# The expert layer of a decoder block: 64 of 256 tokens through fetched expert rows on VectorE, 64 in a stationary block of high and low parts, 128 as before

## The chip, the cores and the metric

One core of a Trainium2 chip runs the whole kernel in one launch. The metric is the device time of that launch in microseconds. The kernel before takes 2736.85 us (median of 3 runs, 2736.78 to 2737.09). The engines are TensorE (PE in the profile, its weight loads PEld), VectorE (DVE), ScalarE (ACT), GpSimd (POOL) and SyncE (SP), which issues most transfers.

## The reference

A decoder block for 256 tokens of width 2048 in float32: a retention branch and a dilated attention, merged by gates; a cross-attention to 256 memory tokens; and an expert layer of 16384 experts, of which each token takes 16 for each of 8 heads. The change is in the last one:

```
def peer_ffn(h, w_q, subkeys, u_tab, v_tab):
    qh = (ht @ w_q).reshape(t, PEER_HEADS, 2, PEER_QUERY_DIM // 2)
    sc = jnp.einsum('thpd,hpnd->thpn', qh, subkeys)
    v_top, i_top = lax.top_k(sc, PEER_TOPK)
    combo = (v_top[:, :, 0, :, None] + v_top[:, :, 1, None, :]).reshape(...)
    c_val, c_idx = lax.top_k(combo, PEER_TOPK)
    ...
    e_idx = i1 * PEER_N_KEYS + i2
    gates = jax.nn.softmax(c_val, axis=-1)
    ...
        u = u_tab[i_]
        a = jax.nn.gelu(jnp.einsum('td,tkd->tk', x_, u), approximate=False)
        return jnp.einsum('tk,tkd->td', a * g_, v_tab[i_])
```

So each token needs 128 rows of `u_tab` and 128 of `v_tab`, each of 2048 numbers (8 KB). Each table has 134 MB.

## The kernel before, in words

All weights are streamed once from HBM in 464 pieces of 1 MB (128 partitions x 4 k-slices x 512 columns). `ahead` (L960) brings each piece in: SyncE loads it into one of 3 raw buffers, ScalarE rounds it to a high part (`hi`, L967), VectorE subtracts that to get the low part (`lo`, L968, the "split"). The left operand, the activations transposed, is kept in high and low parts too. For each k-slice and each block of 128 tokens `mm3` (L201 to L204) adds three products: high by high, high by low, low by high. So a piece is 4 x 2 x 3 = 24 matmuls. The split runs two pieces ahead of TensorE (`SPLIT_AHEAD`).

The order of everything beside the pieces is written by generators. After each piece `tick` (L120) gives each active generator a credit; a generator runs until its yields have used it up. The credit is `TICK` = 4.0 after each piece, and `FINE` = 1.5 twice a piece while the routing runs (`fine`).

The expert layer does not fetch rows. It computes all 16384 experts densely for all 256 tokens. In 128 pieces of `u` (32 chunks of 512 experts) it multiplies the normalized tokens by the table; `evac_u` (L768) applies the Gelu on ScalarE and GpSimd's queue stores the chunk's activations to HBM. Meanwhile VectorE routes: `route_top` and `route_pairs` select the experts and `gate_matrix` (L737) makes, from one-hot rows (L749, L751) and small matmuls (L758), a matrix G of 256 tokens x 16384 gates, mostly zeros, in HBM. `weigh` (L780) reads G and the activations back chunk by chunk, multiplies them on VectorE (L802) and transposes the product with `to_T`; `v_group` (L805) multiplies that by 128 pieces of `v` and adds the sums to the residual rows `x_rows` (L827). The first 80 pieces are of `u` (`RUN_AHEAD` = 20 chunks), then 8 of `v` and 8 of `u` in turn, at the end `v` alone.

Buffers of 4 KB per partition are called `unit`; there are 29 of them, taken from whatever was given back.

Of the kernel before, what the change touches and what calls it, by code (L numbers as in the profile page):

```python
# [33 lines left out]
SPLIT_AHEAD = 2  # L34
N_UNITS = 29
TICK = 4.0
FINE = 1.5

# [33 lines left out]
def block_kernel(ctx, tc, a, out):  # L72
# [73 lines left out]
    def piece(ap, fn):  # L146
        prog.append((ap, fn))
# [506 lines left out]

    G_d = [dp.tile([128, N_EXP], F32, name=f"G{tb}") for tb in range(2)]
    g_done = []

    rt = [{}, {}]

    def route_top(n):  # L660

        while sc_rows[n] is None:
            yield
        for tb in range(2):
            if n == 0:
                u = unit([3, 256])
                rt[tb]["v"] = u[:, 0].rearrange("p (n a) -> p n a", a=16)
                rt[tb]["i"] = u[:, 1].bitcast(U32).rearrange("p (n a) -> p n a", a=16)
                rt[tb]["if"] = u[:, 2].rearrange("p (h s a) -> p h s a", h=8, s=2)
            for i in range(4):  # L670
                top16(rt[tb]["v"][:, 4 * n + i], rt[tb]["i"][:, 4 * n + i], sc_rows[n][:, tb, i], work([128]))
                yield 1.57
        sc_rows[n] = 0

# [38 lines left out]

    def route_gates():
        yield
        yield
        for tb in range(2):
            ex = rt[tb]["g"][0]
            nc.scalar.activation(ex, ex, AF.Exp)
        for tb in range(2):  # L720
            ex, sel, _ = rt[tb]["g"]
            su = sp.tile([128, 2, 8], F32, tag="gsum", name="gsum")
            nc.vector.tensor_reduce(su[:, 0], ex, axis=AX.X, op=OP.add)
            nc.vector.reciprocal(su[:, 1], su[:, 0])
            nc.vector.tensor_tensor(sel[:, 2], ex, bc(su[:, 1, :, None], [128, 8, 16]), op=OP.mult)
        yield
        for tb in range(2):
            _, sel, uc = rt[tb]["g"]
            tp = bank("tp", [3, 128])
            for s in range(3):  # L730
                nc.tensor.transpose(tp[:, s], sel[:, s].rearrange("p h k -> p (h k)"), ident)
            tt = uc[:, 3:6]
            nc.scalar.copy(tt, tp)
            rt[tb] = {"T": tt}
        yield

    def gate_matrix():  # L737
# [3 lines left out]
        prev = None  # L741
        for tb, t0 in [(tb, t0) for tb in range(2) for t0 in range(0, 128, 8)] + [(None, None)]:
            cur = None
# [18 lines left out]
            yield 2.6  # L762
        fine[0] = False
        g_done.extend([0, 1])

    ga = {}

    def evac_u(c, acc):  # L768
        g = unit([2, 512])
        for tb in range(2):  # L770
            nc.scalar.activation(g[:, tb], acc[tb], AF.Gelu, scale=sm["rstd2"][:, tb:tb + 1])  # L771
        d = dp.tile([128, 2, 512], F32, name=f"act{c}")
        nc.gpsimd.dma_start(d, g)  # L773
        ga[c] = d

    A_T = {}
    v_at = [0]
    y_rows = {}

    def weigh():  # L780

        while len(g_done) < 2:
            yield
        w = {}

        def load(c):
            w[c] = unit([2, 512]), unit([2, 512])
            for tb in range(2):
                nc.sync.dma_start(w[c][0][:, tb], G_d[tb][:, c * 512:c * 512 + 512])
            nc.sync.dma_start(w[c][1], ga.pop(c))  # L790

        yield
        yield
        load(0)
        for c in range(N_CH):
            while (c + 1 < N_CH and c + 1 not in ga) or c > 2 * v_at[0] + 3:
                yield
            if c + 1 < N_CH:
                load(c + 1)
            yield  # L800
            m, g = w.pop(c)
            nc.vector.tensor_mul(g, g, m)  # L802
            yield from to_T(g, A_T, c)

    def v_group(gi):  # L805
        accs = {}
        for n in range(4):
            for c2 in range(2):
                def fn(hi, lo, n=n, c2=c2):
                    c = 2 * gi + c2  # L810
                    v_at[0] = gi
                    wait(lambda: c in A_T)
                    if c2 == 0:
                        accs[n] = [bank("acc", [512]) for _ in range(2)]
                    th, tl = A_T[c]
                    for k in range(4):
                        for tb in range(2):
                            s = slice(tb * 128, tb * 128 + 128)
                            mm3(accs[n][tb], th[:, k, s], tl[:, k, s], hi[:, k], lo[:, k],
                                c2 == 0 and k == 0, c2 == 1 and k == 3)  # L820
                    if n == 3:
                        del A_T[c]
                    if c2 == 1:
                        acc = accs.pop(n)
                        r = x_rows[n]
                        for tb in range(2):
                            nc.vector.tensor_add(r[:, tb], r[:, tb], acc[tb])  # L827
# [92 lines left out]
    def route():  # L920
        for n in range(4):
            yield from route_top(n)
        for tb in range(2):
            yield from route_pairs(tb)
        yield from route_gates()
        yield from gate_matrix()
    call(lambda: add(route()))
    call(lambda: add(weigh()))
    chunks(a["w_pq"], hf_T, KQ, late, evac_rows_T(pq_T, "rstd2"))

    def u_chunk(c):
        chunks(a["u"][c * KQ:c * KQ + KQ], hf_T, KQ, straight(0, 1), lambda _, acc: evac_u(c, acc))

# [125 lines left out]
def _layout(inputs):  # L1059
# [33 lines left out]
```

## Time and profile before

| | |
|---|---|
| median of 3 runs | 2736.85 us |
| the profiled execution: its time, and its span | 2736.54 us, 2734.7 us |
| TensorE busy | 2715.8 us (99%) |
| VectorE busy | 1691.2 us (62%) |
| ScalarE busy | 1160.0 us (42%) |
| GpSimd busy | 116.4 us (4%) |
| granted clock of TensorE, mean | 0.999 |
| bytes moved, mean rate | 580 MB, 212 GB/s |

The expert layer's pieces run from about 1245 us to the end. Three views are used below. The page groups instructions by line: busy time, mean duration, and the idle time of the engine before them with what ended it. The windows give busy time of every engine in a stretch, the share of time that the 16 transfer engines were busy, and GB/s. The timeline shows single instructions; two neighbouring ones of an engine overlap by a little, so what an instruction costs a full engine is the distance of two starts.

### The profile page before, as it was taken

The page shows a single profiled execution, that of the slowest core. Times are in us where ns is not written, and L with a number is a line of the kernel's source. Part 1 is how long each engine was busy: PE and PEld are TensorE (multiplying, and loading weights), DVE is VectorE, ACT ScalarE, POOL GpSimd, SP SyncE. Part 2 cuts the span into 40 slices and gives each one's busy share as a digit, 9 for nine tenths or more (in the row PEclk, how much of TensorE's full clock was granted, in tenths as well). Part 3 has the DMA queues.
Part 4 walks back from the last instruction along what each step waited for, and adds up shares of the span by engine and source line. Part 5 has one row for each costly group of instructions (what it writes and reads, how often), then busy time and mean ns, then how long its engine had stood idle before and what let it go on. Part 6 is the DMA issues. An engine that isn't in the chain of part 4 may idle for free.

```text
span 2734.7 us, 31099 instructions
## 1 busy us (share of the span) xinstructions
PE 2715.8 (99%) x12642; PEld 2266.7 (83%) x12642; DVE 1691.2 (62%) x2115; ACT 1160.0 (42%) x1047; POOL 116.4 (4%) x125
## 2 busy tenths in 40 slices
PE   9999999999999999999999999999999999999998
PEld 7888888888888888888888888888888888888886
DVE  7566447886554444569998885445555455666664
ACT  6444334443464443444445444333344334333333
POOL 1211110002000000000000000000000000000001
PEclk9999999999999999999999999999999999999999
DMA  8554554567575444545667777565666566666663
GB/s 294 193 178 170 187 190 177 193 240 255 187 264 189 171 156 156 183 171 198 218 216 238 241 242 281 211 224 214 223 232 239 206 224 231 248 218 248 233 229 123
DMA packets 127951, 580.48 MB, mean 212 GB/s; under 512 B 11200, under 2 KB 43968, under 8 KB 68928
## 3 DMA queue, kind: packets, MB, share of 16 engines
q1 hardware_dynamic: 118096, 543.23, 56.1%
q0 software_dynamic: 9712, 35.26, 3.4%
q8 instruction: 99, 1.62, 0.2%
q14 instruction: 44, 0.36, 0.0%
HBM read 538.61 MB, written 39.85 MB: 212 GB/s over the span
## 4 chain that ended last, share of the span: by engine, by line
PE 98%; POOL 1%; DVE 1%; issue 0%; DMA 0%; POOLq 0%; SPq 0%; ACT 0%; DVEq 0%
PE acc L202 30%; PE acc L204 30%; PE acc L203 30%; PE tp L185 2%; PE sm L758 2%; POOL unit L332 1%; PE sm L584 1%; PE sm L615 1%; PE sm L456 0%; PE sm L478 0%; DVE work L326 0%; PE sm L640 0%; DVE work L330 0%; DMA raw<-in_w_in_dram 0%; PE tp L472 0%
## 5 line engine op out<-in xcount | busy, mean ns | idle before, releaser
L968 DVE TENSOR_TENSOR lo<-raw,hi 128x2048 fp32r<-128x2048 f32 (+1 forms) x464 | 1060.1, 2286 | 822.7 <-ACT hi L967 819.0
L202 PE MATMUL acc<-hi,unit 128*128 128x512 f32 x3712 | 1458.4, 393 | 6.3 <-ACT hi L987 6.3
L204 PE MATMUL acc<-hi,unit 128*128 128x512 f32 x3712 | 1445.9, 390 | 0.0
L203 PE MATMUL acc<-lo,unit 128*128 128x512 f32 x3712 | 1445.5, 389 | 0.0
L967 ACT CAST hi<-raw 128x2048 fp32r<-128x2048 f32 (+1 forms) x464 | 881.8, 1902 | 885.6 <-PE acc L204 767.9
L202 PEld LDWEIGHTS acc<-hi,unit 128*128 128x128 f32 x3712 | 697.5, 188 | 146.6 <-ACT hi L987 6.3
L204 PEld LDWEIGHTS acc<-hi,unit 128*128 128x128 f32 x3712 | 697.0, 188 | 145.7
L203 PEld LDWEIGHTS acc<-lo,unit 128*128 128x128 f32 x3712 | 697.6, 188 | 141.7 <-DVE lo L988 0.9
L827 DVE TENSOR_TENSOR unit<-unit,acc 128x512 f32<-128x512 f32 x128 | 87.5, 687 | 28.2 <-PE acc L204 27.7
L190 ACT CAST unit<-tp 128x512 fp32r<-128x512 f32 x76 | 40.9, 590 | 142.7 <-PE tp L185 142.7
L191 DVE TENSOR_TENSOR unit<-tp,unit 128x512 fp32r<-128x512 f32 x76 | 48.9, 685 | 75.3 <-ACT unit L190 75.3
L749 DVE TENSOR_SCALAR unit<-iota,unit 128x128 f32<-128x128 f32 x256 | 88.4, 345 | 0.0
L771 ACT ACTIVATE unit<-acc,rstd 128x512 f32<-128x512 f32 x64 | 43.8, 690 | 81.6 <-PE acc L204 81.6
L185 PE MATMUL tp<-ident,unit 128*128 128x128 f32 x544 | 71.8, 273 | 1.4 <-POOL unit L332 1.4
L751 DVE TENSOR_SCALAR unit<-iota,unit 128x128 f32<-128x128 f32 x256 | 73.0, 285 | 0.0
L185 PEld LDWEIGHTS tp<-ident,unit 128*128 128x128 f32 x544 | 63.1, 140 | 11.5 <-POOL unit L332 3.5
L759 ACT COPY unit<-sm 128x512 f32<-128x512 f32 x64 | 37.6, 588 | 79.3 <-PE sm L758 67.3
L773 POOL DMA_DIRECT2D act<-unit x32 | 17.1, 535 | 1109.0 <-ACT unit L771 1109.0
L758 PEld LDWEIGHTS sm<-unit 128*128 128x128 f32 x512 | 62.0, 191 | 2.5
L758 PE MATMUL sm<-unit 128*128 128x128 f32 x512 | 62.2, 275 | 0.0
L389 DVE RECIPROCAL unit<-unit 128x256 f32<-128x256 f32 x32 | 56.1, 1754 | 1.1
L188 ACT COPY unit<-tp 128x512 f32<-128x512 f32 x44 | 23.7, 592 | 59.2 <-PE tp L185 59.2
(183 smaller groups left out, 772.4 us busy)
## 6 DMA issues: line engine op xcount, KB each, us to landing
raw<-in_u_dram SPq DMA_DIRECT2D x128, 1024.0 KB, 4.8
raw<-in_v_dram SPq DMA_DIRECT2D x128, 1024.0 KB, 4.8
raw<-in_w_in_dram SPq DMA_DIRECT2D x96, 1024.0 KB, 4.7
raw<-in_w_kv_dram SPq DMA_DIRECT2D x32, 1024.0 KB, 4.7
raw<-in_w_out_dram SPq DMA_DIRECT2D x16, 1024.0 KB, 4.7
raw<-in_w_qm_dram SPq DMA_DIRECT2D x16, 1024.0 KB, 4.8
raw<-in_w_om_dram SPq DMA_DIRECT2D x16, 1024.0 KB, 4.7
raw<-in_w_pq_dram SPq DMA_DIRECT2D x16, 1024.0 KB, 4.8
```

The source lines that it names most:

```text
L185: nc.tensor.transpose(tp[:, k, tb * 128:tb * 128 + 128], rows[:, tb, f:f + 128], ident)
L191: nc.vector.tensor_sub(lo[:, s], tp, hi[:, s])
L202: nc.tensor.matmul(acc, lh, rh, start=start, stop=False)
L203: nc.tensor.matmul(acc, lh, rl, start=False, stop=False)
L204: nc.tensor.matmul(acc, ll, rh, start=False, stop=stop)
L389: nc.vector.reciprocal(rows[:, tb, c], rows[:, tb, c])
L749: nc.vector.tensor_scalar(cur[0][:, i], iota, it[:, 0, t], it[:, 2, t], op0=OP.is_equal, op1=OP.mult)
L751: nc.vector.tensor_scalar(cur[1][:, i], iota, it[:, 1, t], None, op0=OP.is_equal)
L758: nc.tensor.matmul(p[:, i], lh[:, 4 * j + i], rh[:, 4 * j + i], start=True, stop=True)
L827: nc.vector.tensor_add(r[:, tb], r[:, tb], acc[tb])
L967: nc.scalar.copy(hi[:, ks], raw[:, ks])
L968: nc.vector.tensor_sub(lo[:, ks], raw[:, ks], hi[:, ks])
```

## The change

The 256 tokens are no longer treated alike in the expert layer.

- Tokens 0 to 127 are computed densely as before, with three matmuls per k-slice.
- Tokens 128 to 191 are computed densely with high and low parts side by side in one 128-wide stationary block. `side_by_side` copies the low parts of these 64 tokens into the columns of the high parts of tokens 192 to 255. Per k-slice two matmuls (block by high, block by low) give sums whose upper and lower 64 partitions are added in the evacuation, with a ScalarE copy between partition halves and a VectorE addition (L876, L877 of the changed kernel). `evac_u` now stores from ScalarE's queue, in two parts.
- Tokens 192 to 255 (`LANES`) leave the dense computation. `lanes_in` makes their normalized rows, `lanes` does their experts on VectorE. A token takes two partitions, each with 64 of its 128 experts, and a row is handled in two halves of 1024 numbers, so there are 128 steps for `u` and 128 for `v`. A step fetches 128 half rows, one per partition, by an indirect transfer of GpSimd's queue; it is then one VectorE instruction: a TENSOR_TENSOR_REDUCE for the dot product with the token's row, or a SCALAR_TENSOR_TENSOR that adds the weighted row to the sum. Fetches are issued 3 steps ahead (`ROWS_AHEAD`). A step's yield costs 0.8 of a piece's credit (`LANE_STEP`), so 5 steps go with 4 pieces. The sums come into the residual rows in the last but one group of `v_group`.
- Routing is done for tokens 128 to 255 first, so that the row steps can start; `gate_matrix` has 64 + 128 tokens. There is one more unit buffer.

The diff, cut to what is spoken of:

```
-N_UNITS = 29
+N_UNITS = 30
+LANES = slice(64, 128)
+LOW = slice(0, 64)
+LANE_STEP = 0.8
+ROWS_AHEAD = 3
...
-        for tb, t0 in [(tb, t0) for tb in range(2) for t0 in range(0, 128, 8)] + [(None, None)]:
+        for tb, t0 in [(1, t0) for t0 in range(0, 64, 8)] + [(0, t0) for t0 in range(0, 128, 8)] + [(None, None)]:
...
+    def lanes(sel):
...
+        def fetch(i):
+            if i < 256:
+                rows[i] = unit([1024])
+                t = a["u_rows" if i < 128 else "v_rows"]
+                j = i % 128
+                nc.gpsimd.indirect_dma_start(rows[i], None, t, bass.IndirectOffsetOnAxis(
+                    ap=ix[:, j // 2, j % 2:j % 2 + 1], axis=0))
+
+        def turn():
+            return LANE_STEP * (2 * FINE if fine[0] else TICK)
...
+        for i in range(128):
+            r = rows.pop(i)
+            nc.vector.tensor_tensor_reduce(r, r, hn[i % 2].rearrange("p a b -> p (a b)"), 1.0, 0.0, OP.mult, OP.add,
+                                           dots[:, i // 2, i % 2:i % 2 + 1])
+            del r
+            fetch(i + ROWS_AHEAD)
+            yield turn()
...
+        for i in range(128):
+            r = rows.pop(128 + i)
+            y = ys[i % 2].rearrange("p a b -> p (a b)")
+            nc.vector.scalar_tensor_tensor(y, r, coef[:, i // 2:i // 2 + 1], y, op0=OP.mult, op1=OP.add)
+            del r
+            fetch(128 + i + ROWS_AHEAD)
+            yield turn()
...
     def evac_u(c, acc):
-        g = unit([2, 512])
-        for tb in range(2):
-            nc.scalar.activation(g[:, tb], acc[tb], AF.Gelu, scale=sm["rstd2"][:, tb:tb + 1])
-        d = dp.tile([128, 2, 512], F32, name=f"act{c}")
-        nc.gpsimd.dma_start(d, g)
+        g = work([512])
+        nc.scalar.activation(g, acc[0], AF.Gelu, scale=sm["rstd2"][:, 0:1])
+        d = dp.tile([128, 512], F32, name=f"act{c}")
+        nc.scalar.dma_start(d, g)
         ga[c] = d
+        own, other = (LANES, LOW) if c % 2 else (LOW, LANES)
...
+        nc.scalar.copy(w[own], acc[1][other])
+        nc.vector.tensor_add(w[own], w[own], acc[1][own])
+        nc.scalar.activation(b[own], w[own], AF.Gelu, scale=sm["rstdB"][own])
...
+                for k in range(4):
+                    first, last = kq == 0 and k == 0, kq == KQ - 1 and k == 3
+                    mm3(accs[0], th[:, k, 0:128], tl[:, k, 0:128], hi[:, k], lo[:, k], first, last)
+                    nc.tensor.matmul(accs[1], th[:, k, 128:256], hi[:, k], start=first, stop=False)
+                    nc.tensor.matmul(accs[1], th[:, k, 128:256], lo[:, k], start=False, stop=last)
...
     def v_group(gi):
...
                     for k in range(4):
-                        for tb in range(2):
-                            s = slice(tb * 128, tb * 128 + 128)
-                            mm3(accs[n][tb], th[:, k, s], tl[:, k, s], hi[:, k], lo[:, k],
-                                c2 == 0 and k == 0, c2 == 1 and k == 3)
+                        f, e = c2 == 0 and k == 0, c2 == 1 and k == 3
+                        mm3(accs[n][0], ta[:, 0, k], ta[:, 1, k], hi[:, k], lo[:, k], f, e)
+                        nc.tensor.matmul(accs[n][1], tb[:, k], hi[:, k], start=f, stop=False)
+                        nc.tensor.matmul(accs[n][1], tb[:, k], lo[:, k], start=False, stop=e)
...
+    def side_by_side(kq):
+        hi, lo = hf_T[kq]
+        nc.scalar.copy(hi[:, :, 192:256], lo[:, :, 128:192])
```

How the order moves, at three places. First TensorE in a piece of `u` past the 80th: one k-slice before, where acc_14853 is tokens 0 to 127 and acc_14854 tokens 128 to 255 (unit_7702 holds high parts of the activations, unit_7703 low ones):

```order
L202 MATMUL acc_14853<-hi_14879,unit_7702 128x512
L203 MATMUL acc_14853<-lo_14880,unit_7702 128x512
L204 MATMUL acc_14853<-hi_14879,unit_7703 128x512
L202 MATMUL acc_14854<-hi_14879,unit_7702 128x512
L203 MATMUL acc_14854<-lo_14880,unit_7702 128x512
L204 MATMUL acc_14854<-hi_14879,unit_7703 128x512
```

and the same now (acc_11873 and acc_11874; unit_7703 high, unit_7704 low):

```order
L206 MATMUL acc_11873<-hi_11899,unit_7703 128x512
L207 MATMUL acc_11873<-lo_11900,unit_7703 128x512
L208 MATMUL acc_11873<-hi_11899,unit_7704 128x512
L900 MATMUL acc_11874<-hi_11899,unit_7703 128x512
L901 MATMUL acc_11874<-lo_11900,unit_7703 128x512
```

The sixth matmul is gone; the low parts of tokens 128 to 191 stand in the columns of unit_7703.

Second VectorE in the pieces of `u` and `v` after the routing. Before, the splits (`lo`) stand alone but for a few rows at the end of a group, where `v`'s sums are added (L827) and a chunk is weighted (L802):

```order
L968 TENSOR_TENSOR lo_14513<-raw_14424,hi_14512 128x2048
L968 TENSOR_TENSOR lo_14548<-raw_14456,hi_14547 128x2048
L968 TENSOR_TENSOR lo_14585<-raw_14486,hi_14584 128x2048
L827 TENSOR_TENSOR unit_4861<-unit_4861,acc_14553 128x512
L827 TENSOR_TENSOR unit_4861<-unit_4861,acc_14554 128x512
L802 TENSOR_TENSOR unit_14112<-unit_14112,unit_14111 128x1024
```

Now, with unit_13567 and unit_13568 the two sums of the fetched rows, unit_9055 the weights, and the third name a fetched row:

```order
L1145 TENSOR_TENSOR lo_14162<-raw_14073,hi_14161 128x2048
L877 TENSOR_TENSOR work_14192<-work_14192,acc_14076 64x512
L853 SCALAR_TENSOR_TENSOR unit_13568<-unit_14101,unit_9055,unit_13568 128x1024
L1145 TENSOR_TENSOR lo_14200<-raw_14107,hi_14199 128x2048
L853 SCALAR_TENSOR_TENSOR unit_13567<-unit_14130,unit_9055,unit_13567 128x1024
L853 SCALAR_TENSOR_TENSOR unit_13568<-unit_14159,unit_9055,unit_13568 128x1024
L1145 TENSOR_TENSOR lo_14234<-raw_14136,hi_14233 128x2048
```

One row step, and at every fourth piece two, stands between two splits, and L877, for which ScalarE waits in `evac_u`, stands among them.

Third GpSimd's queue in the same stretch. Before it held the activation stores:

```order
L773 DMA act12_11025<-unit_11022 128x1024 [waits DMASW0_49,Activation_49]
L773 DMA act13_11312<-unit_11309 128x1024 [waits DMASW1_49,Activation_49]
L773 DMA act14_11567<-unit_11564 128x1024 [waits DMASW2_49,Activation_49]
L773 DMA act15_11772<-unit_11769 128x1024 [waits DMASW3_49,Activation_49]
L773 DMA act16_11932<-unit_11929 128x1024 [waits DMASW4_49,Activation_49]
```

Now it holds the fetches of rows:

```order
L824 DMA unit_13812<-in_v_rows_dram,unit_9055 128x1024 [waits DMASW2_49,DVE_49]
L824 DMA unit_13815<-in_v_rows_dram,unit_9055 128x1024 [waits DMASW3_49,DVE_49]
L824 DMA unit_13847<-in_v_rows_dram,unit_9055 128x1024 [waits DMASW4_49,DVE_49]
L824 DMA unit_13889<-in_v_rows_dram,unit_9055 128x1024 [waits DMASW5_49,DMAHW2_49,PE_49,Activation_49]
L824 DMA unit_13921<-in_v_rows_dram,unit_9055 128x1024 [waits DMASW7_49,DMASW6_49,DVE_49]
```

A fetch waits for the engine that last used its unit buffer, mostly VectorE with an earlier row step, at times TensorE or a store.

More of the change, by code (lines that the diff above doesn't have):

```diff
@@ L231, in chunks @@
             piece(wap[n * nk + kq], make(n, kq, c == 0, c == nk - 1))
+            if after is not None and n == 3:
+                call(lambda kq=kq: after(kq))
     def straight(n0, n1, nk=KQ):
@@ L777, in block_kernel, with u_chunk, make, fn @@
+    A_T, B_T = {}, {}
     v_at = [0]
     y_rows = {}
+    def u_chunk(c):
+        accs = []
+        def make(kq):
+            def fn(hi, lo):
+                wait(lambda: "rstdB" in sm)
+                if kq == 0:
+                    accs.extend(bank("acc", [512]) for _ in range(2))
+                th, tl = hf_T[kq]
+                for k in range(4):
[3 more added lines that the diff above has]
+                    nc.tensor.matmul(accs[1], th[:, k, 128:256], lo[:, k], start=False, stop=last)
+                    if k == 1 and fine[0]:
+                        tick()
+                if kq == KQ - 1:
+                    evac_u(c, accs)
+            return fn
+        for kq in range(KQ):
+            piece(a["u"][c * KQ + kq], make(kq))
@@ new lines, in weigh @@
+            A_T[c] = o
+            if c % 2 == 0:
+                continue
+            t = w.pop("b")
+            nc.vector.tensor_mul(t[:, 1], t[:, 1], t[:, 0])
+            yield
+            tp = bank("tp", [4, 128])
+            for k in range(4):
+                nc.tensor.transpose(tp[:, k], t[:, 1, k * 128:k * 128 + 128], ident)
+            o = unit([2, 4, 128], F32R)
+            both = tp.rearrange("p k (c t) -> p c k t", c=2)
+            for j in range(2):
+                nc.scalar.copy(o[:, j, :, 0:64], both[:, j])
+                nc.vector.tensor_sub(o[:, j, :, 64:128], both[:, j], o[:, j, :, 0:64])
@@ L805, in v_group, with evac @@
+            B_T[c // 2] = o
     def v_group(gi):
         accs = {}
+        last = gi == N_CH // 2 - 1
+        def evac(n, acc):
+            r = x_rows[n]
+            nc.vector.tensor_add(r[:, 0], r[:, 0], acc[0])
+            if not last:
+                nc.vector.tensor_add(r[:, 1], r[:, 1], acc[1])
+                if gi == N_CH // 2 - 2:
+                    w = work([512])
+                    nc.scalar.copy(w[LOW], r[LANES, 1])
+                    nc.vector.tensor_add(r[LOW, 1], r[LOW, 1], w[LOW])
+                    wait(lambda: "ys" in sm)
+                    nc.scalar.copy(r[LANES, 1], sm["ys"][n // 2][LANES, n % 2])
+                return
+            w = work([512])
+            nc.scalar.copy(w[LOW], acc[1][LANES])
+            nc.vector.tensor_add(r[LOW, 1], r[LOW, 1], acc[1][LOW])
+            nc.vector.tensor_add(r[LOW, 1], r[LOW, 1], w[LOW])
+            y_rows[n] = unit([2, 512]) if n < 3 else r
+            for tb in range(2):
+                j = work([512])
+                nc.scalar.activation(j, r[:, tb], AF.Square, accum_out=ssq3[:, tb, n:n + 1])
+                if n < 3:
+                    nc.gpsimd.tensor_mul(y_rows[n][:, tb], r[:, tb], g_fin[n // 2][:, n % 2])
@@ L928, in block_kernel @@
     call(lambda: add(weigh()))
[L929 to L932 removed]
+    call(lambda: add(lanes_in()))
+    def side_by_side(kq):
+        hi, lo = hf_T[kq]
+        nc.scalar.copy(hi[:, :, 192:256], lo[:, :, 128:192])
+    chunks(a["w_pq"], hf_T, KQ, late, evac_rows_T(pq_T, "rstd2"), side_by_side)
     call(lambda: fine.__setitem__(0, True))
```

187 lines of the change are left out of this document (129 added, 58 removed).

## The prediction

> **What bounds the kernel now.** I read the page first, then busy time by stage, then single instructions in the stages that the change touches. The page's first lines and its chain of waits:
>
> ```profile
> span 2734.7 us, 31099 instructions
> PE 2715.8 (99%) x12642; PEld 2266.7 (83%) x12642; DVE 1691.2 (62%) x2115; ACT 1160.0 (42%) x1047; POOL 116.4 (4%) x125
> ...
> PE 98%; POOL 1%; DVE 1%; issue 0%; DMA 0%; POOLq 0%; SPq 0%; ACT 0%; DVEq 0%
> PE acc L202 30%; PE acc L204 30%; PE acc L203 30%; PE tp L185 2%; PE sm L758 2%; POOL unit L332 1%; PE sm L584 1%; PE sm L615 1%; PE sm L456 0%; PE sm L478 0%; DVE work L326 0%; PE sm L640 0%; DVE work L330 0%; DMA raw<-in_w_in_dram 0%; PE tp L472 0%
> ```
>
> TensorE is the chain: it hardly waits for anybody, so the time is the number of matmuls times their spacing. The spacing is not the 0.39 us of a row but the distance of two starts. TensorE in the timeline, two rows that are 24 matmuls (one weight piece) apart:
>
> ```profile
> 1786.03 0.39 PE L202 MATMUL acc<-hi,unit 128*128 128x512 f32 x1
> ...
> 1791.47 0.39 PE L202 MATMUL acc<-hi,unit 128*128 128x512 f32 x1
> ```
>
> 5.44 us for 24, 0.2267 us each. The expert layer has 256 of the 464 pieces. I cut its time where the changed program's order changes character: 65 pieces with routing and gate matrix (stage A, 1245 to 1660 us of before), 160 pieces (stage B, to 2551), the rest (stage C). Busy time by stage:
>
> ```profile
> core 0: us, PE busy (x) PEld busy (x) DVE busy (x) ACT busy (x) POOL busy (x), PEclk, DMA share, GB/s
> 1245.00:1352.00 107.00, 107.00 (x482) 88.91 (x481) 100.47 (x234) 44.14 (x32) 2.18 (x4) 1.00 0.59 207
> 1352.00:1660.00 308.00, 308.00 (x1621) 264.61 (x1620) 259.01 (x670) 143.08 (x140) 6.43 (x12) 1.00 0.73 235
> 1660.00:2551.00 891.00, 891.00 (x4036) 739.85 (x4035) 494.12 (x333) 351.16 (x244) 8.50 (x16) 1.00 0.63 229
> 2551.00:2735.00 184.00, 172.46 (x785) 142.92 (x783) 105.85 (x86) 67.10 (x60) 9.41 (x9) 0.98 0.54 198
> ```
>
> In A VectorE is already busy 87% (359 of 415 us); in B it has room (55%), and the transfers too (229 GB/s). The change takes work from TensorE and gives it to just these two.
>
> **The change part by part.**
>
> *Fewer matmuls.* Per k-slice the second accumulator gets two matmuls of a 128-wide block in place of three, of the same shape as now: 20 in place of 24 per piece, 4 x 0.2267 = 0.91 us. Over 256 pieces 232 us less TensorE. The gate matrix loses 64 of 256 tokens; 16 matmuls of it in the chain:
>
> ```profile
> 1460.86 1.78 PE sm L758 x16
> ```
>
> That is 0.111 us each, two per token: 64 x 0.22 = 14 us less. Transposes (the same 128 columns, taken at 0.111) fall from 8 to 6 per chunk. TensorE sums by the order: A 343 us, B 3219 x 0.2267 + 156 x 0.111 = 747, C 136 (before 172, a difference of 36).
>
> *VectorE.* The new rows are 128 TENSOR_TENSOR_REDUCE (each followed by a small instruction that writes its sum out) and 128 SCALAR_TENSOR_TENSOR of 128x1024. None stands in the trace; the nearest are:
>
> ```profile
> L802 DVE TENSOR_TENSOR unit<-unit 128x1024 f32<-128x1024 f32 x32 | 39.0, 1220 | 3.8 <-DMA unit<-act 3.8
> L709 DVE TENSOR_REDUCE unit<-unit 128x64 f32<-128x1024 f32 x8 | 9.8, 1220 | 0.3
> L439 DVE SCALAR_TENSOR_TENSOR unit<-unit,rrs 128x128 f32<-128x128 f32 x16 | 4.4, 348 | 3.6 <-POOL rrs L161 3.6
> L1016 DVE SCALAR_TENSOR_TENSOR unit<-unit,rstd 128x512 f32<-128x512 f32 x2 | 1.4, 743 | 0.0
> ```
>
> The last two give 1.03 ns per element, so 1.27 us at 1024. On a full VectorE an instruction costs the distance of starts, less than its row. VectorE in the timeline:
>
> ```profile
> 1431.21 2.29 DVE L968 TENSOR_TENSOR lo<-raw,hi 128x2048 fp32r<-128x2048 f32 x1 [0.22 <-ACT hi L967]
> 1433.42 0.34 DVE L749 TENSOR_SCALAR unit<-iota,unit 128x128 f32<-128x128 f32 x1
> ...
> 1434.33 0.34 DVE L749 TENSOR_SCALAR unit<-iota,unit 128x128 f32<-128x128 f32 x1
> ...
> 1434.78 0.34 DVE L749 TENSOR_SCALAR unit<-iota,unit 128x128 f32<-128x128 f32 x1
> ```
>
> A split costs 2.21 us, 0.08 less than its row, and a gate pair 0.45. A row step is then 1.14 to 1.19 us, 1.19 taken with the sum's write. Bounds: 1.14, and 2.2 if the reduction walks its row twice.
>
> Stage A on VectorE: 65 splits 144 us, 192 gate pairs 87, 58 row steps 69, the routing that stands there 105 (now 359 - 144 - 256 x 0.45 = 100, and by the order a few instructions more): 405. The row steps come in before the gate matrix is done, so VectorE passes TensorE (343) and A stays as long as it was (415): with 2% for waits of an engine that has no room, 412, **2 us less**.
>
> Stage B on VectorE: 160 splits 354, 198 row steps 236, 96 adds of accumulators at 0.60 (687 ns less 0.08) 58, the rest of the weighting some 57. 705 us, under TensorE's 747.
>
> ```profile
> L968 DVE TENSOR_TENSOR lo<-raw,hi 128x2048 fp32r<-128x2048 f32 x160 | 366.8, 2293 | 323.4 <-ACT hi L967 320.7
> L827 DVE TENSOR_TENSOR unit<-unit,acc 128x512 f32<-128x512 f32 x96 | 65.6, 687 | 13.9 <-PE acc L204 13.6
> ```
>
> *Transfers.* Each row step fetches 128 x 4 KB = 0.524 MB by an indirect transfer. Stage B moves 160 x 1.049 (weights) + 196 x 0.524 (rows) + 29 (G and activations, fewer than now) = 299 MB, against 203 before. What the transfer engines can do when they are full shows in two stretches:
>
> ```profile
> 5.00:25.00 20.00, 18.70 (x74) 14.84 (x75) 16.34 (x32) 16.03 (x33) 0.00 (x0) 1.00 1.02 376
> 768.00:778.00 10.00, 10.00 (x46) 8.28 (x45) 8.69 (x13) 10.00 (x15) 0.79 (x2) 1.00 1.01 396
> ```
>
> A share of 1 is 376 GB/s over 20 us and 396 over 10. At 376, B takes 299/0.376 = 796 us, at 396 756; I take the longer stretch, since B must hold it for 800 us. So the transfers, not TensorE (747) or VectorE (705), bound B. All three lie within 12%, and three raw buffers are little to even them out: 2% more, 812 us, **80 us less** than 892. The bounds are 747 (transfers hidden) and what the second rival takes. The Trainium skill (HBM Reference, Specifications) gives a core about 358 GB/s; by that B would be 836 us. Both rows above lie higher, so the trace does not show that limit here.
>
> *Waits.* A row is fetched three steps ahead, at 1.25 steps per piece and 812/160 = 5.1 us a piece 12 us. The slowest kind of landing of such a size now:
>
> ```profile
> unit<-in_mem_dram POOLq DMA_DIRECT2D x4, 512.0 KB, 10.3
> ```
>
> It just fits. If a row is late, its step holds VectorE, behind it the next split (which TensorE needs) and L877, for which ScalarE waits in evac_u with the next cast behind it. That cast takes 1.9 us:
>
> ```profile
> L967 ACT CAST hi<-raw 128x2048 fp32r<-128x2048 f32 (+1 forms) x464 | 881.8, 1902 | 885.6 <-PE acc L204 767.9
> ```
>
> Cast and split, 4.2 us, have the time of two pieces (10 us), so some 5 us of lateness are covered. The activation stores go from POOL's queue to ScalarE's, 48 issues; a store's issue now costs POOL this:
>
> ```profile
> L773 POOL DMA_DIRECT2D act<-unit x32 | 17.1, 535 | 1109.0 <-ACT unit L771 1109.0
> ```
>
> 26 us at that price over 1300 us, on an engine busy 40% in B: nothing, unless ScalarE has no room. lanes_in, the copies of side_by_side and the shifted adds are a few us beside other work.
>
> *Stage C* has no rows left (they end 30 pieces before the last) and goes as TensorE does: 36 less, 1 back for the longer last evacuation, **35 us less**.
>
> Sum, against the profiled execution's 2736.5 us (span 2734.7; the median of three is 2736.85, 0.3 more, which I leave out): 2736.5 - 2 - 80 - 35 = 2619.5, said as **2620**.
>
> **The rivals.**
>
> *All is hidden.* If transfers come to 400 GB/s and more, TensorE bounds B: A 10, B 145, C 36 less, 2546; with half of the 2% waits 2557. For it: TensorE never waited in before although VectorE was 87% busy. Against: 299 MB in 747 us is 401 GB/s, over both rows.
>
> *The transfers hold less* (this ends slower). Rows scattered over two tables of 134 MB, beside weights, stores and small G packets, may do worse than both rows. With A and C at 37 us less, nothing is gained where B takes 892 + 37 = 929 us, that is at 322 GB/s; at 340 (880 us) the time is 2688, at 310 (966) 2774. This row, where weights and gate loads mix, speaks for it, though its share was not full:
>
> ```profile
> 1665.00:1700.00 35.00, 35.00 (x168) 29.23 (x167) 20.52 (x16) 16.92 (x16) 1.06 (x2) 1.00 0.85 310
> ```
>
> 310/0.85 is 365 at a full share, B 820. Taken at 340: 2688.
>
> *GpSimd holds VectorE up* (slower too). Fetches are issued by POOL, which reads their indices from SBUF. A POOL addition beside a split, and the split in VectorE's timeline:
>
> ```profile
> 221.72 1.28 POOL L372 TENSOR_TENSOR unit<-unit 128x512 f32<-128x512 f32 x1 [0.76 <-DVE unit L371]
> ```
>
> ```profile
> 222.01 3.14 DVE L968 TENSOR_TENSOR lo<-raw,hi 128x2048 fp32r<-128x2048 f32 x1
> ```
>
> 3.14 for 2.29: 0.85 us lost. If each of 256 fetches cost VectorE g, A grows by 60g and B is 705 + 196g: no gain from g = 0.88 on, and at 1.0 us 2736.5 - 2 + 60 + 9 - 35 = 2769. Against it: a plain transfer's issue is 0.54 us, and VectorE's splits beside L773 are not longer. The Trainium skill (SBUF — State Buffer, Who interferes with whom) says that an instruction of VectorE with two SBUF inputs shuts out one of GpSimd that reads SBUF, and the other way round. The two rows agree; whether an indirect issue counts as such no run here shows.
>
> *The reduction walks twice.* 1.07 us more for 128 steps: A + 62, B's first half becomes VectorE's (about + 10): 2692.
>
> **How the numbers follow.** Forecast 0.52 (its own range 2585 to 2655), all hidden 0.17, transfers at 340 or less 0.15 (a third of it at 322 or below, no faster than before), GpSimd 0.08 (half of it above g = 0.88), two walks 0.08. The range 2555 to 2710 takes in the first, most of the second, the two at 2690. About 0.2% (5.5 us) is what a measurement of this kernel can tell from no change. Faster 0.87, same 0.03, slower 0.10.
>
> **What would show it.** Right: in B the DMA share is near 1 at 370 to 390 GB/s, VectorE busy about 90%, pieces 5 us apart, splits released by transfers; in A VectorE over 95% with TensorE waiting; in C pieces 4.5 us apart. Wrong: row steps above 1.4 us, splits of 3 us beside fetches, a chain that runs over POOL, or B below 340 GB/s with VectorE idle behind fetched rows.

## The result and the profile after

The changed kernel takes 2647.11 us (median of 4 runs, 2645.93 to 2647.77), the kernel before 2736.97 (4 runs): a ratio of 0.9671, with a 95% interval of 0.9655 to 0.9688. The forecast was 2620 with a range of 2555 to 2710. So the sign and the range held, and the time lies 27 us above the forecast. The profiled execution took 2646.55 us.

The page of the changed kernel, its engines, the two rows of the transfers in 40 slices, and its chain:

```profile
span 2644.8 us, 29732 instructions
PE 2524.7 (95%) x11426; PEld 2077.2 (79%) x11426; DVE 1964.3 (74%) x2446; ACT 1176.3 (44%) x1084; POOL 573.1 (22%) x361
...
DMA  7555555566575544564676799999999999999874
GB/s 288 201 181 170 181 193 172 179 237 245 207 284 177 191 155 148 178 220 163 207 278 237 250 291 301 337 374 398 393 366 347 394 383 416 361 381 388 302 267 153
...
PE 50%; DVE 20%; DMA 7%; issue 5%; ACT 3%; POOL 0%; SPq 0%; ACTq 0%; DVEq 0%; POOLq 0%
```

TensorE was 98% of the chain before and is 50% now. From the 24th slice to the 37th the transfers are nearly full. Busy time by stage, in the columns of the forecast's table:

```profile
1245.00:1352.00 107.00, 95.11 (x407) 75.86 (x406) 96.05 (x201) 50.03 (x40) 1.03 (x2) 0.95 0.60 207
1352.00:1698.00 346.00, 292.23 (x1313) 235.03 (x1312) 322.86 (x779) 139.52 (x134) 114.14 (x66) 0.92 0.85 284
1698.00:2491.00 793.00, 760.36 (x3365) 621.59 (x3364) 712.33 (x636) 359.24 (x264) 353.56 (x192) 0.98 0.98 375
2491.00:2645.00 154.00, 139.60 (x631) 114.67 (x629) 108.47 (x99) 72.70 (x71) 9.02 (x8) 0.97 0.65 230
```

Cut at the same pieces as in the forecast (by the starts of the splits), the stages are:

| stage | before | forecast | after | after less forecast |
|---|---|---|---|---|
| A, 65 pieces | 414.3 | 412 | 452.7 | +41 |
| B, 160 pieces | 891.6 | 812 | 793.5 | -18 |
| C, the rest | 183.3 | 148 | 153.7 | +6 |

A did not stay as it was: it became 38 us longer. B gained more than forecast, C less. The new instructions, in the page's groups:

```profile
L1145 DVE TENSOR_TENSOR lo<-raw,hi 128x2048 fp32r<-128x2048 f32 (+1 forms) x464 | 1058.7, 2283 | 508.4 <-ACT hi L1144 502.3
...
L824 POOL DMA_INDIRECT unit<-in_u_rows_dram,unit x128 | 226.1, 1766 | 379.1 <-DVE unit L835 173.2
L824 POOL DMA_INDIRECT unit<-in_v_rows_dram,unit x128 | 241.1, 1883 | 251.3 <-DVE unit L853 64.5
...
L853 DVE SCALAR_TENSOR_TENSOR unit<-unit 128x1024 f32<-128x1024 f32 x128 | 161.5, 1277 | 6.8 <-DMA unit<-xs 6.7
L835 DVE CUSTOM_DVE_ANT_0 unit<-unit 128x1024 f32<-128x1024 f32 x128 | 154.6, 1216 | 4.8 <-DMA unit<-in_u_rows_dram,unit 4.7
```

A dot product (L835) takes 1216 ns, a weighted addition (L853) 1277 ns. VectorE stood 4.7 us for a late row of `u` in the whole run, and the 6.7 us before L853 were for the residual rows, not for a fetched one. The splits are as long as before (2283 ns in the row above, 2286 for the same 464 before), though GpSimd now issues 256 fetches of 1.77 and 1.88 us each.

Where did A go? The waits there (engine, what it would do, whom it waits for: us in total, times, longest):

```profile
ACT unit L878 <- DVE work L877: 93.7, 16, 10.5
...
ACT hi L1144 <- PE acc L900: 41.0, 16, 5.4
...
DVE lo L1145 <- ACT hi L1144: 20.5, 16, 2.8
...
DVE unit L835 <- DMA unit<-in_u_rows_dram,unit: 4.7, 1, 4.7
```

ScalarE stood 94 us of 453 inside `evac_u`, and VectorE 20 us for casts that came late. One such place in the timeline of the changed kernel:

```profile
1464.08 0.58 ACT L876 COPY work<-acc 64x512 f32<-64x512 f32 x1 [0.40 <-ACT work L868]
...
1466.02 1.22 DVE L715 TENSOR_REDUCE unit<-unit 128x64 f32<-128x1024 f32 x1
...
1467.16 1.22 DVE L835 CUSTOM_DVE_ANT_0 unit<-unit 128x1024 f32<-128x1024 f32 x1
...
1468.30 0.08 DVE L835 DVE_READ_ACCUMULATOR2_ANT unit<- 128x1 f32 x1
...
1468.30 2.29 DVE L1145 TENSOR_TENSOR lo<-raw,hi 128x2048 fp32r<-128x2048 f32 x1
...
1472.09 1.22 DVE L835 CUSTOM_DVE_ANT_0 unit<-unit 128x1024 f32<-128x1024 f32 x1
...
1473.23 0.08 DVE L835 DVE_READ_ACCUMULATOR2_ANT unit<- 128x1 f32 x1
...
1473.35 0.68 DVE L877 TENSOR_TENSOR work<-work,acc 64x512 f32<-64x512 f32 x1
...
1474.06 0.72 ACT L878 ACTIVATE unit<-work,rstdB 64x512 f32<-64x512 f32 x1 [9.40 <-DVE work L877]
```

The copy L876 ends at 1464.7, so L877 could start there. It stands in VectorE's queue behind routing (L715 and others), two row steps and a split, starts at 1473.35, and ScalarE waits 9.4 us for it with the next cast behind.

VectorE also has more routing in A than it had. The groups of its instructions in A, first before, then after (the rounds that take the best 8 of 128 scores; in the changed kernel also the dot products with the instruction behind each, and the addition of `evac_u`):

```profile
L652 DVE MAX8 unit<-work 128x8 f32<-128x128 f32 x12 | 3.5, 295 | 0.4
```

```profile
L835 DVE CUSTOM_DVE_ANT_0 unit<-unit 128x1024 f32<-128x1024 f32 x58 | 70.2, 1212 | 4.8 <-DMA unit<-in_u_rows_dram,unit 4.7
...
L877 DVE TENSOR_TENSOR work<-work,acc 64x512 f32<-64x512 f32 x16 | 10.9, 684 | 2.2 <-ACT work L876 1.8
...
L658 DVE MAX8 unit<-work 128x8 f32<-128x128 f32 x20 | 5.9, 295 | 0.7
...
L835 DVE DVE_READ_ACCUMULATOR2_ANT unit<- 128x1 f32 x58 | 4.5, 78 | 0.0
```

The selection of 16 from 128 scores stands there 20 times in place of 12. By the groups of all its instructions (two MAX8, two FIND_INDEX8, MATCH_REPLACE8 and the loads) this is 14.6 us more, and L877 is 10.9, both by their rows, which overlap a little.

### The profile page after: what moved, and what is told of

Read it like the earlier page. It is cut to its first block, busy times and chain, and to the rows that moved or that the text cites. A ratio compares the mean times of both kernels' runs of the same rounds, so it can differ in the third digit from the quotient of the medians.

```text
span 2644.8 us, 29732 instructions
## 1 busy us (share of the span) xinstructions
PE 2524.7 (95%) x11426; PEld 2077.2 (79%) x11426; DVE 1964.3 (74%) x2446; ACT 1176.3 (44%) x1084; POOL 573.1 (22%) x361
## 4 chain that ended last, share of the span: by engine, by line
PE 50%; DVE 20%; DMA 7%; issue 5%; ACT 3%; POOL 0%; SPq 0%; ACTq 0%; DVEq 0%; POOLq 0%
PE acc L207 13%; PE acc L208 13%; PE acc L206 13%; DVE lo L1145 8%; DMA raw<-in_v_dram 3%; DVE unit L835 2%; ACT hi L1144 2%; PE acc L1002 2%; PE acc L1003 2%; DVE unit L751 2%; DVE unit L753 1%; DMA raw<-in_u_dram 1%; PE acc L900 1%; PE acc L901 1%; DMA unit<-in_v_rows_dram,unit 1%
## 5 line engine op out<-in xcount | busy, mean ns | idle before, releaser
L1145 DVE TENSOR_TENSOR lo<-raw,hi 128x2048 fp32r<-128x2048 f32 (+1 forms) x464 | 1058.7, 2283 | 508.4 <-ACT hi L1144 502.3
L207 PE MATMUL acc<-lo,unit 128*128 128x512 f32 x2688 | 1059.1, 394 | 34.1 <-DVE lo L1145 33.6
L206 PE MATMUL acc<-hi,unit 128*128 128x512 f32 x2688 | 1069.4, 398 | 15.9 <-ACT hi L1144 9.7
L208 PE MATMUL acc<-hi,unit 128*128 128x512 f32 x2688 | 1054.4, 392 | 0.0
L207 PEld LDWEIGHTS acc<-lo,unit 128*128 128x128 f32 x2688 | 510.2, 190 | 149.4 <-DVE lo L1145 47.9
L206 PEld LDWEIGHTS acc<-hi,unit 128*128 128x128 f32 x2688 | 510.0, 190 | 120.3 <-ACT hi L1144 12.2
L208 PEld LDWEIGHTS acc<-hi,unit 128*128 128x128 f32 x2688 | 509.5, 190 | 106.3
L824 POOL DMA_INDIRECT unit<-in_u_rows_dram,unit x128 | 226.1, 1766 | 379.1 <-DVE unit L835 173.2
L824 POOL DMA_INDIRECT unit<-in_v_rows_dram,unit x128 | 241.1, 1883 | 251.3 <-DVE unit L853 64.5
L900 PE MATMUL acc<-hi,unit 128*128 128x512 f32 x512 | 204.2, 399 | 0.0
L901 PE MATMUL acc<-lo,unit 128*128 128x512 f32 x512 | 203.6, 398 | 0.0
L1002 PE MATMUL acc<-hi,unit 128*128 128x512 f32 x512 | 200.6, 392 | 0.0
L1003 PE MATMUL acc<-lo,unit 128*128 128x512 f32 x512 | 200.4, 391 | 0.0
L853 DVE SCALAR_TENSOR_TENSOR unit<-unit 128x1024 f32<-128x1024 f32 x128 | 161.5, 1277 | 6.8 <-DMA unit<-xs 6.7
L835 DVE CUSTOM_DVE_ANT_0 unit<-unit 128x1024 f32<-128x1024 f32 x128 | 154.6, 1216 | 4.8 <-DMA unit<-in_u_rows_dram,unit 4.7
L900 PEld LDWEIGHTS acc<-hi,unit 128*128 128x128 f32 x512 | 99.2, 194 | 21.7
L901 PEld LDWEIGHTS acc<-lo,unit 128*128 128x128 f32 x512 | 99.0, 193 | 21.5
L1003 PEld LDWEIGHTS acc<-lo,unit 128*128 128x128 f32 x512 | 96.7, 189 | 20.6
L1002 PEld LDWEIGHTS acc<-hi,unit 128*128 128x128 f32 x512 | 96.7, 189 | 20.6
L338 POOL TENSOR_TENSOR unit<-work 128x512 f32<-128x512 f32 x20 | 37.8, 1888 | 176.4 <-DVE work L336 157.0
```

What stands on the lines that cost most here:

```text
L206: nc.tensor.matmul(acc, lh, rh, start=start, stop=False)
L207: nc.tensor.matmul(acc, lh, rl, start=False, stop=False)
L208: nc.tensor.matmul(acc, ll, rh, start=False, stop=stop)
L824: nc.gpsimd.indirect_dma_start(rows[i], None, t, bass.IndirectOffsetOnAxis(ap=ix[:, j // 2, j % 2:j % 2 + 1], axis=0))
L835: nc.vector.tensor_tensor_reduce(r, r, hn[i % 2].rearrange("p a b -> p (a b)"), 1.0, 0.0, OP.mult, OP.add, dots[:, i // 2, i % 2:i % 2 + 1])
L853: nc.vector.scalar_tensor_tensor(y, r, coef[:, i // 2:i // 2 + 1], y, op0=OP.mult, op1=OP.add)
```

## The experiments

The account to be tested first is the forecast's own: row steps cost A VectorE's time, and B the transfers' time. What A lost could also come from the fetches themselves, or from the dense part without any rows, and B could be bound by something else that takes as long.

**Rows that stay.** The work on VectorE is all there, the transfers are not.

```
-            if i < 256:
+            if ROWS_AHEAD <= i < 256:
+                rows[i] = rows_kept[i % ROWS_AHEAD]
+            elif i < 256:
...
-            nc.vector.tensor_tensor_reduce(r, r, ...
+            nc.vector.tensor_tensor_reduce(spare, r, ...
```

> Leaves out all fetches but the first three: the row steps of VectorE work 256 times on three rows that stay in SBUF. Account 1 (stage A, 65 pieces, is bound by VectorE; stage B, 160 pieces, by transfers at about 375 GB/s): A stays at 445 to 455 us, B falls from 793 to 750 to 765, where TensorE bounds it; the time is about 2610. Account 2 (B is bound by VectorE, 93% busy in its later part): B stays near 790, time 2640 or more. Account 3 (the fetches' issue on GpSimd holds VectorE up in A): A falls by 20 us or more as well.

2613.87 us, ratio 0.9549 (0.9530 to 0.9568). A is 454.4, B 758.6:

```profile
1699.00:2458.00 759.00, 750.59 (x3366) 615.75 (x3365) 711.96 (x639) 358.01 (x264) 0.58 (x1) 1.00 0.75 259
```

Without fetches A is as long as with them, so neither the fetches nor GpSimd's issues are what A lost. B falls by 35 us to TensorE's time (751 busy of 759).

**Fetches only.** The transfers are all there, VectorE's row steps are cut to 8 of 1024 columns.

```
-            nc.vector.tensor_tensor_reduce(r, r, hn[i % 2]...,
+            nc.vector.tensor_tensor_reduce(r[:, 0:8], r[:, 0:8], hn[i % 2]...[:, 0:8],
...
-            nc.vector.scalar_tensor_tensor(y, r, ..., y,
+            nc.vector.scalar_tensor_tensor(y[:, 0:8], r[:, 0:8], ..., y[:, 0:8],
```

> Leaves out most of the row arithmetic: every row is fetched, but each row step works on 8 of its 1024 columns. Account 1: B stays at 780 to 795 us (transfers), A falls by some 58 x 1.1 = 64 us to about 385; time about 2575 to 2585. Account 2: B falls to 750 and with it the time to about 2540. Account 3: A stays above 420.

2579.08 us, ratio 0.9422 (0.9403 to 0.9441). A is 407.9, B 768.4:

```profile
1653.00:2421.00 768.00, 747.57 (x3345) 615.79 (x3344) 511.23 (x636) 358.66 (x263) 279.31 (x193) 0.99 1.00 388
```

The time lies in what account 1 expected, the stages do not: B should have stayed at 780 to 795 and came to 768. The same bytes went at 388 GB/s. So 375 GB/s is not the most that the transfers can hold. A fell by 45 us, where account 1 had some 64.

**No rows at all.** What the dense part costs alone.

```
-            if i < 256:
+            if i < 0:
...
-            nc.vector.tensor_tensor_reduce(...)
...
-            nc.vector.scalar_tensor_tensor(...)
```

> Leaves out the 64 tokens' row work altogether, fetches and row steps; the dense part alone is left. By every account TensorE bounds B: 750 to 760 us; A about 365 to 385, the rest as in the changed kernel; time 2530 to 2545. So the row work costs the changed kernel some 100 to 115 us. If A stays above 420, it is not the row steps that made it longer than forecast, but the routing in its new order.

2545.89 us, ratio 0.9301 (0.9282 to 0.9319), just above what was expected. The stages A (two rows) and B:

```profile
1245.00:1352.00 107.00, 95.17 (x410) 76.01 (x409) 95.28 (x197) 50.05 (x41) 1.04 (x2) 0.95 0.60 206
1352.00:1644.00 292.00, 270.43 (x1309) 222.06 (x1308) 256.62 (x667) 140.47 (x135) 0.00 (x0) 0.96 0.72 224
1644.00:2389.00 745.00, 744.18 (x3357) 615.70 (x3356) 489.83 (x370) 358.37 (x263) 1.12 (x2) 1.00 0.76 264
```

B is TensorE's, 744 of 745; the forecast's count was 747. A is 399, where 365 to 385 was expected, although TensorE has 366 and VectorE 352 of it: neither engine's sum sets it. The rows add 54 us to that, less than the forecast's 69. So most of A's miss is in the dense part. Cut where the first gate pair starts, A splits into routing and gate matrix; the two lines behind them are waits in the whole of A (the Gelu is L871 here, the cast L1137, the split L1138):

```profile
1245.00:1482.00 237.00, 206.06 (x854) 162.20 (x853) 208.99 (x450) 105.29 (x84) 1.04 (x2) 0.94 0.60 203
1482.00:1627.00 145.00, 142.54 (x789) 121.84 (x787) 135.34 (x409) 75.21 (x83) 0.00 (x0) 0.99 0.82 241
```

```profile
ACT unit L871 <- DVE work L870: 56.7, 16, 7.4
...
DVE lo L1138 <- ACT hi L1137: 35.9, 20, 3.1
```

The gate matrix is TensorE's, 143 of 145 us. In the routing TensorE is busy 206 and VectorE 209 of 237, and 21 of VectorE's 36 us of waiting for casts lie there, with 50 of ScalarE's 57 at the Gelu.

**A slower pace**, so that VectorE has fewer row steps per piece.

```
-LANE_STEP = 0.8
+LANE_STEP = 0.87
```

> LANE_STEP 0.87 here takes four more ticks at the end than 0.85 would; one row step per 0.87 piece credits, so the rows run to the last group but one. Account 1: some 17 rows move from A and B into the last pieces, where transfers and VectorE have room: 5 x 1.2 + 12 x 1.4 = 23 us less, 2620 to 2630, if the last rows don't come too late; if they do, the last group but one waits and the gain is under 10.

2655.29 us (2648.02 to 2661.85), ratio 0.9697 (0.9675 to 0.9720): 8 us longer than the changed kernel by the medians. A 450.1, B 790.9, and C 169 in place of 154:

```profile
2486.00:2655.00 169.00, 143.86 (x639) 117.94 (x637) 132.74 (x120) 75.33 (x73) 31.46 (x18) 0.93 0.67 246
```

The expectation for rows that end too late was a gain under 10; it is a loss. TensorE, busy 140 of 154 in the changed kernel, is busy 144 of 169: rows are still fetched (9 of the 18 operations of GpSimd), and 20 row steps lie in C, where the changed kernel has none. The few microseconds won in A and B are given back there. That the last group but one has to wait for the sums of these rows is the likely reason; it is not shown, since none of the longest waits of C is for them.

**The second block's Gelu later.** It and its store are given out one step later, when VectorE's addition is done; `weigh` then also waits for the store.

```
-        nc.scalar.activation(b[own], w[own], AF.Gelu, scale=sm["rstdB"][own])
-        if c % 2:
-            d = dp.tile([128, 512], F32, name=f"actb{c}")
-            nc.scalar.dma_start(d, b_part.pop(0))
-            gb[c // 2] = d
+        def finish():
+            yield
+            nc.scalar.activation(b[own], w[own], AF.Gelu, scale=sm["rstdB"][own])
+            if c % 2:
+                d = dp.tile([128, 512], F32, name=f"actb{c}")
+                nc.scalar.dma_start(d, b)
+                gb[c // 2] = d
+        add(finish())
...
-            while (c + 1 < N_CH and c + 1 not in ga) or c > 2 * v_at[0] + 3:
+            while (c + 1 < N_CH and (c + 1 not in ga or c % 2 == 0 and c // 2 not in gb)) or c > 2 * v_at[0] + 3:
```

> The Gelu of the second block (L878) and the store behind it are given out one step later, when VectorE's addition L877 is done, so that ScalarE goes on with casts; nothing is left out. Account H (part of stage A's miss is ScalarE held behind L877: it waited 94 us there, casts came late and VectorE stood 20 us for them): ScalarE's wait at this Gelu falls below 30 us, A falls from 453 to 425-435, B by 0-5, the time is 2617-2632. Account S (A is simply VectorE's sum, 419 us busy of 453, the wait lies beside it): A stays at 443-453 and the time at 2637-2648, the wait moving to another line.

2625.96 us (2623.36 to 2630.70), ratio 0.9598 (0.9582 to 0.9614): 21 us less than the changed kernel. A is 440.0, B 781.6. Waits in A (the Gelu is L881 here, the cast L1148, the split L1149):

```profile
ACT unit L881 <- DVE work L877: 50.3, 12, 8.8
...
DVE lo L1149 <- ACT hi L1148: 7.7, 6, 2.3
```

VectorE's wait for casts fell by 12.8 us, and A by 12.7. So account H holds in kind, but only a third of A's miss goes with it: one step later is often still too early (50 us of waiting remain). B gained 12, where 0 to 5 was expected.

**Rows only after the gate matrix.** Stage A has next to none (3 of the 256 steps), and they come at 1.49 per piece.

```
-LANE_STEP = 0.8
+LANE_STEP = 0.67
...
-        while len(hn) < 2:
+        while len(hn) < 2 or len(g_done) < 2:
```

> Fetched rows start only when the gate matrix is done, and at 1.49 steps per piece in place of 1.25 (LANE_STEP 0.67); nothing is left out. Account 1 (a row step costs stage A VectorE time, stage B transfer time): A falls to the 399 of the kernel without rows; the 256 steps then lie over 172 pieces, 344 MB at 375 GB/s = 918 us, and 22 pieces at 4.5 us remain: 1247 + 399 + 918 + 100 = 2664, between 2654 and 2674. Account 2 (stage B isn't transfers alone, its pieces could take more rows beside TensorE): below 2640. Account 3 (A is late by its waits, rows or not): A above 430.

2633.82 us (2629.51 to 2639.88), ratio 0.9629 (0.9612 to 0.9645). This is account 2's side (below 2640), not account 1's (2654 to 2674). Account 3 falls too, since A is 405.2. B is 818.2:

```profile
1650.00:2468.00 818.00, 766.01 (x3364) 619.81 (x3364) 755.43 (x731) 355.87 (x260) 446.86 (x243) 0.98 1.01 396
```

With 40 row steps more, B takes only 25 us more, 0.6 us each; at 375 GB/s the bytes alone would be 0.524/0.375 = 1.4 us each. The transfers hold 396 GB/s over 818 us. So bytes at 375 GB/s are not what a row step costs B.

**The third matmul put back** in the second block, beside the row work, the reverse half of the change.

```
-                    nc.tensor.matmul(accs[1], th[:, k, 128:256], hi[:, k], start=first, stop=False)
-                    nc.tensor.matmul(accs[1], th[:, k, 128:256], lo[:, k], start=False, stop=last)
+                    mm3(accs[1], th[:, k, 128:256], th[:, k, 128:256], hi[:, k], lo[:, k], first, last)
```

> The second block gets a third matmul per k-slice again (a repeat of the first, so its sums are not the block's), the fetched rows stay as they are. Account 1 (TensorE's removed matmuls pay all of the gain; with them back it bounds stages B and C): B 160 x 24 x 0.2267 + 21 = 891, C 183-190, A as VectorE sets it, 453-470, together 2770-2795, slower than before. Account 2 (transfers bound B and the matmul was beside them): B stays below 820, the time below 2690.

2784.13 us, ratio 1.0170 (1.0150 to 1.0191), 1.7% slower than before. A 460.3, B 894.8, C 183.7, all as account 1 had it:

```profile
1705.00:2600.00 895.00, 890.47 (x3996) 736.73 (x3994) 722.99 (x637) 359.90 (x263) 337.25 (x193) 1.00 0.89 333
```

What the change added costs 47 us here, nearly all in A (46), and TensorE's removed matmuls are worth 137 us (2784.1 less 2647.1).

**Later Gelu and a pace between.**

```
-LANE_STEP = 0.8
+LANE_STEP = 0.84
...
(and the later Gelu)
```

> The Gelu given out later as in the kernel with that edit alone, and LANE_STEP 0.84 (1.19 steps per piece, the rows end some 15 pieces later, still ahead of the last group but one). Account 1 (B is transfers): B has 9 rows and 5 MB less, 10-12 us, and C takes them beside TensorE: 5 to 12 us below the kernel with the later Gelu alone. If the pace doesn't matter: within 4 us of it.

2612.53 us (2609.31 to 2615.99), ratio 0.9540 (0.9524 to 0.9556): 13 us below the later Gelu alone by the medians, 8 by the profiled executions, of which A and B give 3.5 and 3.6. The pace helps; that B's bytes are the reason is not shown, since B gave a third of what they would.

**Later Gelu and late rows** together (both edits above).

> Both edits at once: the Gelu of the second block given out one step later, and the rows only after the gate matrix at 1.49 steps per piece; nothing is left out. If the two gains add (21 and 13 us below the changed kernel): 2608-2618, with stage A at 392-400. If the later Gelu gained only because row steps stood in VectorE's queue in stage A, it has nothing to give where they are gone from A: 2628-2636.

2620.24 us (2618.85 to 2621.47), ratio 0.9573 (0.9557 to 0.9589): 6 us below the later Gelu alone and 14 below late rows alone. A is 384.6, 21 below the 405.2 of late rows alone and below the 399 of the kernel without rows: the later Gelu pays in A where there are next to no row steps. B is 828, 10 longer than with late rows alone. The time lies between the two expectations: of gains of 34 us together 27 are left.

**Four raw buffers**, and its control.

```
-RAW_BUFS = 3
-N_UNITS = 30
+RAW_BUFS = 4
+N_UNITS = 28
```

> Four raw buffers in place of three, paid for with two unit buffers (28); the order of the instructions is the same, nothing is left out. Account T (the ceiling of the transfers, 375 GB/s, sets stage B): B stays at 785-800, the time within 10 of the changed kernel's. Account U (the ceiling is 390-400 as in the kernels with late rows and with fetches only; B lies above it because TensorE, VectorE and the transfers, all near full, hold one another up through three buffers): B falls to 760-780, the time to 2615-2635.

```
-N_UNITS = 30
+N_UNITS = 28
```

> 28 unit buffers with the three raw buffers as they were: the control for the kernel with four. The order is the same, so within 6 of the changed kernel if units are not short; 10-30 slower if fetched rows or activations wait for a unit, and then the kernel with four raw buffers is read against this one.

With four raw buffers 2625.62 us (2625.07 to 2628.11), ratio 0.9593 (0.9577 to 0.9609); the control 2652.29 (2650.32 to 2653.52), ratio 0.9687 (0.9671 to 0.9703). So the fourth buffer is worth 27 us, and nearly all of it lies in B: 772.1 against 796.9, while A is 453.1 against 454.7. What ScalarE waits for in B, first in the control, then with four buffers:

```profile
ACT hi L1144 <- DMA raw<-in_v_dram: 158.5, 59, 9.5
ACT hi L1144 <- DMA raw<-in_u_dram: 53.4, 22, 7.7
```

```profile
ACT hi L1144 <- DMA raw<-in_v_dram: 14.4, 7, 4.6
```

```profile
1698.00:2471.00 773.00, 755.89 (x3370) 619.25 (x3369) 712.05 (x639) 358.81 (x264) 394.45 (x193) 0.99 0.99 386
```

212 us of waiting for weights become 14, with the same bytes at 386 GB/s. Account U holds in its times: with three buffers, not with the rate that the transfers can reach, B came to 797. How the engines hold one another up through the buffers is argued, and shown only by these waits.

**All that helped**: later Gelu, pace 0.84, four raw and 28 unit buffers.

> The Gelu of the second block given out one step later, LANE_STEP 0.84, four raw buffers and 28 unit buffers; nothing is left out. The parts alone stand at 2612.5 (first two) and at 22-27 us below the kernel with three raw buffers (the last two). If they free different waits they add: 2584-2594, with stage B at 750-760, TensorE's own 747. If the later Gelu and the fourth buffer pay for the same late casts in B, less is left: 2595-2612.

2594.88 us (5 runs, 2592.90 to 2602.52), ratio 0.9478 (0.9465 to 0.9491): faster than both kernels, 142 us less than before and 52 less than the changed one. It stands on the line between the two expectations: of the fourth buffer's 27 us, 18 are left here. In its profiled execution, the longest of the five, A is 435.6 and B 765.1 (750 to 760 was expected if the gains add), so what remains above TensorE is again mostly A.

## Why the prediction was right, and where it was not

*Stage A (the step that failed).* The forecast summed VectorE to 405, added 2% for waits and said that A stays at 412. It is 452.7. VectorE was busy 96.05 + 322.86 = 419 us, 14 more than the sum: the routing, counted at 105 (what stands there before, and 5), has 14.6 us of selections that stood ahead of A before, and the 10.9 of L877, one of the additions that the forecast put at a few us (by their rows; by the distances of starts less). The row steps came to 70 + 4.5 by their rows, near the 69. And VectorE stood idle 34 us, not 8, 20 of them for late casts. The waiting of ScalarE had been named in the forecast, but counted as covered by the time of two pieces, some 5 us; in A its single waits at the Gelu reached 10.5 us. The later Gelu shows this as one cause, worth 13 us in A with the rows and 21 without them.

The kernel without rows shows where the sum broke. A is 399 there, over the sums of both engines. Taking the busier engine of each stretch, 209 us of routing, 143 of gate matrix and 17 for the rest, gives 369, so that the two engines take turns explains little. The other 30 us lie nearly all in the routing, 237 us long, where neither engine is full and VectorE waits 21 us for casts. The same is seen by pieces: the first 16 pieces of A take 88 us before and 92 after, with or without rows, although 16 x 0.91 = 15 us were taken from TensorE. The forecast's own table had the sign: in its first 107 us VectorE was already busy 100. How much of the routing's loss is late casts and how much a granted clock of 0.94 there is not settled.

*Stage B (right in size, only half in reason).* The forecast had 796 us of transfers at 376 GB/s and 2% more; B took 793.5 at 375. That looks like the term itself, but 376 is no ceiling: 386, 388 and 396 GB/s were held over some 800 us by the kernels with four buffers, with fetches only and with late rows. The row from which it came, 5 to 25 us, takes in the start of the transfers, 3 us at 201 GB/s. The middle of that stretch, with weights and the input on SyncE's queue and nothing else:

```profile
8.00:23.00 15.00, 15.00 (x64) 12.04 (x63) 13.88 (x28) 13.89 (x29) 0.00 (x0) 1.00 1.05 405
```

At 396 the same 297 MB (375 x 793) take 750 us, about TensorE's time. No engine alone sets B. Without rows it is 744; VectorE's steps alone add 15, the transfers alone 24, both together 49. The forecast's ceiling was too low, its 2% for three raw buffers too small, and the two errors nearly cancel: that part of the agreement is luck. The fourth buffer gives 25 us of the difference back. Luck, too, is that B's 18 us below the forecast make up for part of A's 41 above it.

*Stage C (a size).* 148 forecast, 153.7 measured: TensorE is busy 139.6 there, near the counted 136; what the other 14 us are was not tested.

*The new instructions.* The row step's price was right: 1.14 us from the dot product's start to that of the split behind it, 1.26 where L877 follows (both in the timeline above), 1.19 taken. The fetches three steps ahead were in time (4.7 us of waits). GpSimd has 467 us of issues, at three times the price of the plain issue in the forecast, and nothing was late for it.

*The rivals.* "All is hidden" gave 2546 to 2557; the kernel without rows takes 2546, so that is what perfect hiding would be, and the best version stays 49 us above it. (The forecast says that its range takes in most of this rival; from 2555 on it takes in only the end.) "The transfers hold less" fell: 375 GB/s and more. "GpSimd holds VectorE up" fell: splits of 2283 ns, and A is the same without the fetches (454). "The reduction walks twice" fell: 1216 ns.

## What to carry to other kernels

When work moves from a full engine to others, sum each stage by short windows, count dependent instructions at their whole row, and ask which engine's in-order queue now holds up a third engine. Three engines within a tenth of one another do not overlap for nothing: two small costs that each hide nearly alone added up to 49 us, and one more buffer was the cheapest cure. A share of the transfer engines near 1 does not prove that they are the bound: move the same bytes with one buffer more before believing it.

## What the runs showed of the hardware

The rate of the transfers at a full share, that is GB/s over the DMA share, differs from stage to stage. It is 229/0.63 = 363 GB/s in B before and 259/0.75 = 345 with rows that stay, but 375/0.98 = 383 in the changed kernel, 396/1.01 = 392 with late rows and 333/0.89 = 374 with the third matmul. The fetched rows are not needed for the higher rate: from 8 to 23 us of the kernel before, with weights and the input coming through one queue, it is 405/1.05 = 386. Why the stages differ, no run tells. The Trainium skill (HBM Reference, Specifications) gives about 358 GB/s as the share of a core when both cores of a pair stream, and about 425 for a core that streams alone. One core runs here, and the 375 to 405 GB/s of the full stretches lie between; the forecast's estimate of 836 us for B used the figure for two.

The issue of an indirect fetch of 128 rows of 4 KB took GpSimd 1.77 to 1.88 us in the mean. VectorE's splits, which have two inputs, did not get longer beside it: from stage A on, the 140 of the changed kernel that overlap such an issue took 2288 ns in the mean, the 114 others 2286. The dot product with its sum came as two instructions, 1216 and 79 ns. In the timeline above the small one starts once together with the split behind it and costs nothing, and once 0.12 us ahead of L877.
